# Splitting the last 4 MB store of an instance-norm kernel into 120 and 8 partitions

## The chip, the cores and the metric

The kernel runs on one core of one Trainium2 chip. The metric is device microseconds of one execution. Executions of one kernel mostly agree within 0.2% (the six of before lie within 0.13%), so a few microseconds can be told apart with several runs, and one microsecond only inside a trace. Times below are medians of the runs named, and times since the start of the span where they have four digits before the point.

## The reference

```python
x = np.random.randn(256, 256, 4096).astype(np.float32); eps = 1e-5
mean = np.mean(x, axis=2, keepdims=True)
var = np.var(x, axis=2, keepdims=True)
out = (x - mean) / np.sqrt(var + eps)
```

65536 rows of 4096 floats, each normalized by itself: 1.07 GB in, 1.07 GB out.

## The kernel before

The rows are cut into 128 tiles of 128 partitions x 4 rows x 16 KB (8 MB). Three tile buffers rotate. SyncE issues all loads and stores, VectorE and ScalarE share the arithmetic. The first and the last tile are stored in halves (2 rows of each partition, 32 KB, 4 MB in all), so that the first half leaves while the second is still computed.

```python
def take(engine, sem, count):
    engine.wait_ge(sem, count)
    engine.sem_clear(sem)

def store_half(s, t, h):                 # one DMA over all 128 partitions
    r = half_of(h)
    take(S, second(done, s, h), half)
    S.dma_start(out=out_t[t][:, r, :], in_=X[s][:, r, :]).then_inc(second(stored, s, h), 16)
# ... (cut) the end of SyncE's program:
load(last % BUFS, last)
store((last - 2) % BUFS, last - 2)
store((last - 1) % BUFS, last - 1)
store_half(last % BUFS, last, 0)
store_half(last % BUFS, last, 1)
for s in ((last - 2) % BUFS, (last - 1) % BUFS, last % BUFS, BUFS):
    take(S, stored[s], 16)
```

`last` is 127, `half` is 2, `BUFS` is 3, `K` is 4. `stored[BUFS]` counts the increments of the last half store. "Ring" below is one of the core's sixteen DMA engines with its queue of packets. An increment is what one ring adds to a DMA's semaphore when its share has landed: here 16 for each whole DMA, one per ring (4144 for the 259 transfers of before). The tiles lie in SBUF, the on-chip memory.

Two words have a narrower sense. A "port" is the place at which packets of different rings are supposed to hold one another up. And a ring's number is a name, since the traces do not number the rings: 0 to 7 are the rings of a store of 8 partitions, 15 is the one that a store of 120 leaves out, and ring k is the one that a store of k + 1 partitions has and a store of k has not. That the rings of a smaller store are among those of a larger one is assumed, not shown.

## Time and profile before

| | value | from |
|---|---|---|
| time | 4964.76 us, median of 6 (4962.69 to 4969.12) | runs beside the changed kernel |
| data moved | 2147.5 MB at 433 GB/s | the page's DMA rows |
| issue of the last store | 4943.18 | timeline |
| its sixteen increments | eight at 10.9 to 11.0 us after the issue, the last at 15.76 us | trace |
| last increment to end of span | 1.4 us | trace |

The prediction shows the lines behind these. One more view of before is needed for what follows, the rings' work after the last issue (columns: stretch, its length, busy time of VectorE, ScalarE and GpSimd, TensorE clock, share of the time that the rings held packets, and the data rate):

```profile
core 0: us, DVE busy (x) ACT busy (x) POOL busy (x), PEclk, DMA share, GB/s
4944.20:4949.00 4.80, 0.00 (x0) 0.00 (x0) 0.00 (x0) 1.00 1.00 430
4949.00:4953.80 4.80, 0.00 (x0) 0.00 (x0) 0.00 (x0) 1.00 0.90 389
4953.80:4959.00 5.20, 0.00 (x0) 0.00 (x0) 0.00 (x0) 1.00 0.18 76
```

For 9.6 us the rings are full or nearly so and move data at close to the rate of the whole body (433 GB/s); then for 5 us only stragglers work. Those 5 us are what the change goes after.

### The profile page before, as it was taken

To read this page: it belongs to the slowest core of one execution; us is meant where nothing else is said; L and a number is where in the kernel's file an instruction comes from. 1 tells how busy PE (TensorE), PEld (TensorE's weight loads), DVE (VectorE), ACT (ScalarE), POOL (GpSimd) and SP (SyncE) were. 2 spreads that over 40 slices of the span, in tenths; PEclk is the share of its full clock that TensorE was granted. 3 is DMA by queue.
4 is the path that set the end of the run, shared out by engine and by line. 5 is a ranking of instruction groups with operands and counts; after the bars stand their busy time and mean duration, and the time that the engine had idled before them with its cause. 6 is when DMAs were issued, how large, how long until landed. Compare 5 with 4: busy or idle time off the path is not lost.

```text
span 4960.3 us, 6348 instructions
## 1 busy us (share of the span) xinstructions
DVE 3390.1 (68%) x2439; ACT 2505.6 (51%) x1416; POOL 0.2 (0%) x4
## 2 busy tenths in 40 slices
DVE  6766666776677766777667776677666776677766
ACT  5555544555445544555445554455544555455545
POOL 0000000000000000000000000000000000000000
DMA  9999999999999999999999999999999999999999
GB/s 423 431 435 430 431 434 433 433 436 433 433 436 432 434 436 432 435 435 433 437 432 434 436 432 434 436 432 433 437 432 434 435 433 435 435 432 438 432 433 406
DMA packets 37299, 2147.52 MB, mean 433 GB/s; under 512 B 4144, under 2 KB 4144, under 8 KB 4144
## 3 DMA queue, kind: packets, MB, share of 16 engines
q1 hardware_dynamic: 37296, 2147.50, 100.0%
q14 instruction: 3, 0.02, 0.0%
HBM read 1073.74 MB, written 1073.74 MB: 433 GB/s over the span
## 4 chain that ended last, share of the span: by engine, by line
DMA 71%; DVE 19%; ACT 7%; another core or an unknown queue 1%; issue 1%; SPq 0%; ACTq 0%; DVEq 0%
DMA x<-in_x_dram 40%; DMA out_dram<-x 31%; DVE part L89 17%; ACT junk L132 3%; ACT x L140 3%; DVE nsum L91 1%; DVE x L110 1%; DVE nmean L93 1%; ACTq L182 0%; ACT std L137 0%; DVE nbias L102 0%; SPq L159 0%; SPq L154 0%; DVE rstd L100 0%
## 5 line engine op out<-in xcount | busy, mean ns | idle before, releaser
L89 DVE TENSOR_REDUCE part<-x 128x64 f32<-128x4096 f32 x512 | 2258.6, 4411 | 1452.4 <-DMA x<-in_x_dram 1452.4
L132 ACT ACTIVATE junk<-x,nmean 128x4096 f32<-128x4096 f32 x512 | 1883.0, 3678 | 2417.0 <-DVE nmean L93 2417.0
L110 DVE TENSOR_SCALAR x<-x,rstd,nbias 128x4096 f32<-128x4096 f32 x382 | 910.2, 2411 | 37.6 <-DVE nbias L102 16.4
L140 ACT ACTIVATE x<-x,nbias,rstd 128x4096 f32<-128x4096 f32 x130 | 492.2, 3786 | 0.0
L91 DVE TENSOR_REDUCE nsum<-part 128x1 f32<-128x64 f32 x512 | 112.4, 220 | 17.7
L132 ACT ACTIVATION_READ_ACCUMULATOR junk<-x,nmean 128x1 f32 x512 | 95.5, 186 | 0.0
L93 DVE TENSOR_SCALAR nmean<-nsum 128x1 f32<-128x1 f32 x512 | 78.5, 153 | 17.5
L100 DVE RECIPROCAL rstd<-std 128x1 f32<-128x1 f32 (+1 forms) x260 | 41.7, 160 | 17.2 <-ACT std L137 16.5
L102 DVE TENSOR_TENSOR nbias<-nmean,rstd 128x1 f32<-128x1 f32 (+1 forms) x260 | 41.6, 160 | 8.9
L137 ACT ACTIVATE std<-ss,eps_tile 128x1 f32<-128x1 f32 x130 | 38.3, 295 | 15.1
L124 ACT ACTIVATE std<-ss,eps_tile 128x3 f32<-128x3 f32 (+1 forms) x130 | 38.5, 296 | 4.2
L132 ACT ACT_TABLE_LOAD x1 | 1.3, 1283 | 1.2 <-DVE eps_tile L211 1.2
L124 ACT ACT_TABLE_LOAD x1 | 1.3, 1283 | 0.0
L211 DVE MEMSET eps_tile<- 128x1 f32 x1 | 0.1, 59 | 1.0 <-SPq L181 1.0
L248 POOL MEMSET const-uint8-127<- 128x1 uint8 x1 | 0.1, 102 | 0.0
L248 POOL MEMSET const-bfloat16-1.0<- 128x1 bf16 x1 | 0.1, 101 | 0.0
L248 POOL MEMSET const-float32-0.0<- 128x1 f32 x1 | 0.1, 98 | 0.2 <-issue 0.2
L248 POOL MEMSET const-float32-1.0<- 128x1 f32 x1 | 0.1, 98 | 0.0
## 6 DMA issues: line engine op xcount, KB each, us to landing
out_dram<-x SPq DMA_DIRECT2D x4, 4096.0 KB, 18.8
x<-in_x_dram SPq DMA_DIRECT2D x2, 4096.0 KB, 16.7
x<-in_x_dram SPq DMA_DIRECT2D x127, 49.2
out_dram<-x SPq DMA_DIRECT2D x126, 30.5
```

What stands on the lines that cost most here:

```text
L89: mine(V.tensor_reduce(out=part[s][:, r, :], in_=row, axis=AX.X, op=ALU.add))
L91: mine(V.tensor_reduce(out=nsum[s][:, c], in_=part[s][:, r, :], axis=AX.X, op=ALU.add, negate=True))
L93: V.tensor_scalar_mul(out=nmean[s][:, c], in0=nsum[s][:, c], scalar1=1.0 / d).then_inc(means, 1)
L100: mine(V.reciprocal(out=rstd[s][:, c], in_=std[s][:, c]))
L102: mine(V.tensor_mul(out=nbias[s][:, c], in0=nmean[s][:, c], in1=rstd[s][:, c]))
L110: V.tensor_scalar(out=x[:, r, :], in0=x[:, r, :], scalar1=rstd[s][:, c], scalar2=nbias[s][:, c], op0=ALU.mult, op1=ALU.add,).then_inc(dn, 1)
L124: A.activation(out=std[s][:, r0:last], in_=ss[s][:, r0:last], func=AF.Sqrt, bias=eps_tile, scale=1.0 / d).then_inc(stds, 1)
L132: A.activation(out=junk, in_=x[:, r, :], func=AF.Square, bias=nmean[s][:, c], scale=1.0, accum_out=ss[s][:, c]).then_inc(own_a, 1)
L137: A.activation(out=std[s][:, c], in_=ss[s][:, c], func=AF.Sqrt, bias=eps_tile, scale=1.0 / d).then_inc(stds, 1)
L140: A.activation(out=x[:, last - 1, :], in_=x[:, last - 1, :], func=AF.Identity, bias=nbias[s][:, c], scale=rstd[s][:, c]).then_inc(dn, 1)
L211: V.memset(eps_tile, eps).then_inc(ready, 1)
L248: nc = _bacc.Bacc("TRN2", target_bir_lowering=False, num_devices=1)
```

## The change

The intent, as I read it: one ring ends some 5 us after eight of the others. A store of 120 partitions should leave that ring out, and the 8 partitions missing go one each to eight rings that are taken to be early.

```diff
+    edge = nc.alloc_semaphore("edge")
...
                 store_half(last % BUFS, last, 0)
-                store_half(last % BUFS, last, 1)
+                take(S, done[BUFS], half)
+                for p, sem in ((slice(0, 120), stored[BUFS]), (slice(120, P), edge)):
+                    src = X[last % BUFS][p, half:K, :]
+                    S.dma_start(out=out_t[last][p, half:K, :], in_=src).then_inc(sem, 16)
+                take(S, edge, 16)
                 for s in ((last - 2) % BUFS, (last - 1) % BUFS, last % BUFS, BUFS):
                     take(S, stored[s], 16)
```

## The prediction

> **What bounds the kernel now.** I read the page's busy table and DMA rows first, then the chain of waits, then the last 60 us. The page of the kernel before:
>
> ```profile
> span 4960.3 us, 6348 instructions
> DVE 3390.1 (68%) x2439; ACT 2505.6 (51%) x1416; POOL 0.2 (0%) x4
> ...
> DMA  9999999999999999999999999999999999999999
> ...
> q1 hardware_dynamic: 37296, 2147.50, 100.0%
> ...
> HBM read 1073.74 MB, written 1073.74 MB: 433 GB/s over the span
> ```
>
> Neither compute engine is full (68% and 51%), while the sixteen DMA rings are full in every slice and their packets take 100.0% of sixteen engines' span. The kernel moves 2147.5 MB at 433 GB/s, and 2147.5 MB / 433 GB/s is 4960 us, the whole span. So the body is a pure transfer limit, which the change does not touch: the same bytes leave by the same rings. The only thing it can alter is how the last rings run out. That is the end of the program, on SyncE:
>
> ```profile
> start us, us, engine line op out<-in xcount [idle before <-releaser]
> ...
> 4940.05 2.41 DVE L110 TENSOR_SCALAR x<-x,rstd,nbias 128x4096 f32<-128x4096 f32 x1
> 4943.18 0.33 SPq L170 DMA_DIRECT2D out_dram<-x  x1
> ```
>
> ```profile
> SPq L68 <- ACT x L140: 16.5, 1, 16.5
> SPq L68 <- DMA out_dram<-x: 15.3, 2, 9.7
> ```
>
> ```profile
> issues: line engine op xcount, KB each, median us to landing
> out_dram<-x SPq DMA_DIRECT2D x1, 4096.0 KB, 15.8
> ```
>
> The last arithmetic ends near 4943.1, the last store is issued at 4943.18, and after it SyncE does nothing but wait for stores: 15.3 us in two waits, the longer 9.7 us (5.7 us for the first half of the last tile, then 9.7 us for the second). It lands 15.8 us after its issue, at 4958.94; the remaining 1.4 us to 4960.3 are closing barriers. How busy the rings are in that stretch:
>
> ```profile
> core 0: us, DVE busy (x) ACT busy (x) POOL busy (x), PEclk, DMA share, GB/s
> 4944.20:4953.80 9.60, 0.00 (x0) 0.00 (x0) 0.00 (x0) 1.00 0.95 410
> 4953.80:4954.30 0.50, 0.00 (x0) 0.00 (x0) 0.00 (x0) 1.00 0.61 262
> 4954.30:4955.80 1.50, 0.00 (x0) 0.00 (x0) 0.00 (x0) 1.00 0.20 87
> 4955.80:4957.40 1.60, 0.00 (x0) 0.00 (x0) 0.00 (x0) 1.00 0.19 82
> ```
>
> Until 4953.8 the rings are nearly all busy (0.95), then they run out one after another. No view prints single semaphore increments, but the trace records them. The sixteen increments of this store come at 4954.10 to 4954.22 (eight rings), then 4954.96, 4955.55, 4955.61, 4955.64, 4957.10, 4957.40, 4957.53 and 4958.94. So the end is one ring, 4.84 us behind the eight that had caught up and 1.41 us behind the next. Its packet records show eight packets of 32 KB back to back from 4948.79 to 4958.47, 1.21 us each, and 0.47 us to the increment; it was still draining the first half when the others started on the second. Eight rings by contrast were idle for some 3 us before the first packet of the last store at 4944.01, that is 0.83 us after its issue. Over the run one ring falls behind steadily (the last increment of a store trails the first by 1.1 us at 219 us, 6.7 us at 920 us, 7.4 us at 4630 us, 8.2 us at the last but one store). The change aims at that ring.
>
> [...] each of the 259 transfers has 16 increments, 4144 in all, the page's count of packets under 512 B. Nothing before shows 120 or 8.
> [...] The trace has one steadily late ring, but does not number the rings, so it cannot say that it is 15.
> [...] sixteen rings reach 433 GB/s together, 27 GB/s each, which is what 32 KB in 1.21 us gives; it shows no transfer of another shape.
>
> **The change part by part.**
> It removes one store of 128 partitions x 32 KB. [...]
> It adds a store of 120 partitions: fifteen rings with eight packets each, 9.7 us again; ring 15 gets none. It adds a store of 8 partitions: one packet on each of rings 0 to 7, 1.21 us more there, queued behind the first. Bytes stay 4 MB. Increments go from 16 to 15 + 8, so the count of tiny packets should rise from 4144 to 4151.
> SyncE: one more issue (the present one took 0.33 us, and the next instruction came 0.38 us after it started). The second issue at about 4943.6 comes while rings 0 to 7 have some 10 us of packets ahead of them, so it lies beside the transfer. One more wait and clear, a clear being 0.025 us in the trace, about 0.05 us, also hidden where the main store ends later.
> The path that sets the end is the last ring. With unchanged rates:
> if the late ring is 15, its end falls to that of its first half, 4949.27, and the next ring decides: 4957.53, or, if one of the three rings at 4957.1 to 4957.5 is among 0 to 7 (likely: each is with chance about one half), that plus 1.21, at most 4958.74. Gain 0.2 to 1.4 us;
> if the late ring is among 8 to 14, nothing changes, 0;
> if it is among 0 to 7, it gets a ninth packet, 4958.94 + 1.21 = 4960.15, loss 1.2 us.
> I give these 0.4, 0.25 and 0.35, since somebody who writes 120 + 8 aims at ring 15[...]. The sum is 0.4 x (-0.5) + 0 + 0.35 x 1.2 = +0.2 us: nothing.
>
> **The rivals.**
> A, ports (chance 0.35): with 120 partitions the engines may get eight neighbouring partitions each. [...] Rings that start together would share a port and each run at half rate: 19.4 us in place of 9.7. [...] Eight rings start together[...]: the end goes from 4958.94 to about 4944.0 + 19.4 + 0.4 = 4963.8, +4.8 us. The eight-partition store is worse off: [...] 4 x 1.21 = 4.8 us, not 1.21, so up to +9.7 us where both meet. I take +5 to +10, middle +7. [...]
> B, interleaved partitions (chance 0.1): if engine e takes partitions e, e+15, e+30 and so on, fifteen rings read fifteen neighbours at a time[...]. 3.93 MB at 4 x 27 GB/s is 36 us, about +27 us. That is still only 0.5% of the time.
> C, the wait moves (small): SyncE waits for the 8-partition store first and for the others after. As all waits must pass, their order changes nothing; the last landing decides. The closing barriers stay 1.4 us.
> D, the transfer is hidden anyway: it isn't for the late ring, since nothing else runs after 4943.2; but for seven of the rings there are 1.4 to 4.8 us of slack, which is what the extra packet of the eight-partition store would live in.
>
> **Range and chances.** Base 4965.49 us, three runs from 4963.85 to 4969.12, so the noise is larger than the change's sum in the plain case. Plain case (0.55): 4965.7. Ports (0.35): 4965.5 + 7 = 4972.5. Interleaved (0.1): 4992. The middle of that mixture lies a little above the base; I say 4967.0. Eight in ten: 4962.5 (full gain of 1.4 us and a good run) to 4976 (ports with both meetings). A 2% step is 99 us, six times what the whole tail after the last issue lasts (15.8 us): the change cannot take out more than that, and even the interleaved rival adds 27. Faster 0.004, same 0.991, slower 0.005.
>
> **What would show each step.** In the changed kernel's page: DMA rings still 9 in every slice and 433 GB/s; tiny packets 4151 and hardware packets 37303 if fifteen and eight rings are right (4160 and 37312 if both still use sixteen). The last part of 3840 KB should land 14.3 to 15.8 us after its issue and that of 256 KB not later than about 16.5 us in the plain case; over 20 us for either, with packets of 2.4 us in place of 1.21, would show the ports, and over 35 us the interleaving. In the increments of the 3840 KB store, no ring at 4.8 us behind would show that the late one was number 15. What would make the prediction wrong: the store of 8 partitions taking much longer than one packet per ring, a lateness that differs so much from run to run that single runs say nothing, or a different drift of the rings over the 4900 us ahead of the changed lines, which would have to be noise, since not one instruction there has changed.

## The result, and the profile after

| | before | after |
|---|---|---|
| median of 6 | 4964.76 us | 4972.54 us (4970.92 to 4973.28) |
| last store's (first) issue to its last increment | 15.76 us | 24.02 us |
| last increment to end of span | 1.4 us | 1.6 us |

The change costs 7.8 us by the medians. The ratio of the fast runs is 1.0014, with a 95% interval of 1.0001 to 1.0027: a small slowdown, far inside 2%. (A ratio is the mean time of one kernel's fast runs over that of the other's in the same rounds, so not quite the ratio of the medians.) The lines of the changed kernel's page that answer to those shown of before:

```profile
span 4970.6 us, 6350 instructions
...
DVE 3390.9 (68%) x2439; ACT 2505.5 (50%) x1416; POOL 0.2 (0%) x4
...
DMA packets 37307, 2147.52 MB, mean 432 GB/s; under 512 B 4152, under 2 KB 4152, under 8 KB 4152
...
q1 hardware_dynamic: 37303, 2147.50, 100.0%
```

Same arithmetic, same bytes, same body. The packets of the hardware queue are 37303, seven more than before: sixteen increments became fifteen and eight. (4152 small packets are those 4151 and one of the instruction queue.) The two profiled spans differ by 10.3 us and not 7.8, because this run reached the last store 1.74 us later, at 4944.92 against 4943.18, before anything that was changed: run to run noise. The tail of the changed kernel, SyncE's two issues merged, then its waits:

```profile
4944.92 1.37 SPq L210 DMA_DIRECT2D out_dram<-x  x2
```

```profile
SPq L69 <- DMA out_dram<-x: 22.7, 1, 22.7
```

```profile
issues: line engine op xcount, KB each, median us to landing
out_dram<-x SPq DMA_DIRECT2D x1, 3840.0 KB, 22.2
out_dram<-x SPq DMA_DIRECT2D x1, 256.0 KB
```

One wait of 22.7 us took the place of two of 15.3 us together. The larger part lands 22.2 us after its issue where the whole store took 15.8. (The view gives no landing for the 256 KB; the increments in the trace put it 23.56 us after its own issue.) Where the time went shows in the rings' view of the changed kernel, to be read against that of before:

```profile
core 0: us, DVE busy (x) ACT busy (x) POOL busy (x), PEclk, DMA share, GB/s
4946.00:4951.00 5.00, 0.00 (x0) 0.00 (x0) 0.00 (x0) 1.00 0.95 229
4951.00:4956.00 5.00, 0.00 (x0) 0.00 (x0) 0.00 (x0) 1.00 0.87 210
4956.00:4961.00 5.00, 0.00 (x0) 0.00 (x0) 0.00 (x0) 1.00 0.91 236
4961.00:4966.00 5.00, 0.00 (x0) 0.00 (x0) 0.00 (x0) 1.00 0.51 151
```

Until 4961 the rings hold packets 0.87 to 0.95 of the time, about as before (1.00 and 0.90), but move 210 to 236 GB/s in place of 430 and 389. The busy share alone would show no fault: a packet that crawls counts as busy. The packet records say the same. All of the last store's packets of 32 KB took 1.21 to 1.26 us before. Of the 136 packets that start after 4945.7 in the changed kernel, 52 take 2.4 to 2.6 us, 43 still 1.21 to 1.3, most others something between; four take 4.4 to 4.9 us, among them the last two of the late ring's first half (4.56 and 4.39 us).

### The profile page after: what moved, and what is told of

Read it like the earlier page. It is cut to its first block, busy times and chain, and to the rows that moved or that the text cites. A ratio compares the mean times of both kernels' runs of the same rounds, so it can differ in the third digit from the quotient of the medians.

```text
span 4970.6 us, 6350 instructions
## 1 busy us (share of the span) xinstructions
DVE 3390.9 (68%) x2439; ACT 2505.5 (50%) x1416; POOL 0.2 (0%) x4
## 2 busy tenths in 40 slices
DMA packets 37307, 2147.52 MB, mean 432 GB/s; under 512 B 4152, under 2 KB 4152, under 8 KB 4152
## 3 DMA queue, kind: packets, MB, share of 16 engines
q1 hardware_dynamic: 37303, 2147.50, 100.0%
## 4 chain that ended last, share of the span: by engine, by line
DMA 73%; DVE 18%; ACT 7%; another core or an unknown queue 1%; issue 1%; SPq 0%; ACTq 0%; DVEq 0%
DMA x<-in_x_dram 41%; DMA out_dram<-x 32%; DVE part L90 16%; ACT junk L133 3%; ACT x L141 3%; DVE nsum L92 1%; DVE nmean L94 1%; DVE x L111 0%; ACTq L183 0%; ACT std L138 0%; SPq L155 0%; SPq L160 0%; ACTq L69 0%; DVE nbias L103 0%
## 6 DMA issues: line engine op xcount, KB each, us to landing
out_dram<-x SPq DMA_DIRECT2D x1, 3840.0 KB, 22.2
x<-in_x_dram SPq DMA_DIRECT2D x127, 49.2
out_dram<-x SPq DMA_DIRECT2D x126, 30.5
```

## The experiments

The theory, the prediction's rival A (called PORT in the expectations): with 120 partitions rings meet in pairs at a port, and each runs at half rate. Against it stand the memory side (the rows that a ring writes also changed), the count (a store on fewer than sixteen rings, the nine packets where eight were, or a second issue and semaphore), and the question whether there is a late ring 15 at all. All eleven kernels gave correct results.

**One shape at a time (m1_shapes).** Behind all waits of the kernel before, ten transfers, each waited for. The first and second write wrong rows, later ones put them right.

```diff
+    for src, dst in ((0:32:4, 120:128), (120:128, 0:128:16), (120:128, 120:128), (0:16:4, 0:4),
+                     (0:4, 0:4), (0:64, 0:64), (0:120, 0:120), (0:128, 0:128)):     # written out one by one
+        S.dma_start(out=out_t[last][dst, half:K, :], in_=X[last % BUFS][src, half:K, :]).then_inc(edge, 16)
+        take(S, edge, 16)
+    # then loads of 0:128 and 0:120 into the same buffer, in the same way
```

> After all stores of the kernel before have landed, ten single transfers run one at a time, each waited for, rings otherwise idle; each packet is 32 KB, 1.21 us alone, and a landing costs some 1.3 us on top (0.83 us to the first packet, about 0.4 after the last). Three theories. PORT[...]: 8 partitions in steps of 4[...] 2.5 us; partitions 120-127 to spread rows 6.1; partitions 120-127 to their own rows 6.1; 4 partitions in steps of 4 2.5; partitions 0-3 6.1; partitions 0-63 11; 0-119 20.7; all 128 11 us. MEMORY (the rows of the HBM side decide, not the partitions): first 6.1, second 2.5, third 6.1. COUNT (what costs is a store on fewer than sixteen rings, or its issue, and a packet is always 1.21 us): every store of 4 or 8 partitions about 2.5, 0-63 6.2, 0-119 11, all 128 11 us. The two loads at the end, 128 and 120 partitions: 11 and 11 if only reads of SBUF suffer, 11 and about 20 if writes do too.

SyncE's timeline in this kernel; since each transfer is waited for, the distance from one start to the next is the time that it took, with some 0.1 us for the wait:

```profile
start us, us, engine line op out<-in xcount [idle before <-releaser]
...
4959.60 0.81 SPq L209 DMA_DIRECT2D out_dram<-x  x1
4962.71 0.31 SPq L211 DMA_DIRECT2D out_dram<-x  x1
4969.07 0.28 SPq L213 DMA_DIRECT2D out_dram<-x  x1
4975.39 0.64 SPq L215 DMA_DIRECT2D out_dram<-x  x1
4978.34 0.26 SPq L217 DMA_DIRECT2D out_dram<-x  x1
4984.62 0.55 SPq L219 DMA_DIRECT2D out_dram<-x  x1
4996.61 0.34 SPq L221 DMA_DIRECT2D out_dram<-x  x1
5017.86 0.37 SPq L223 DMA_DIRECT2D out_dram<-x  x1
5029.08 0.37 SPq L225 DMA_DIRECT2D x<-in_x_dram  x1
5041.55 0.35 SPq L227 DMA_DIRECT2D x<-in_x_dram  x1
```

With the last increments and packet times of the trace:

| transfer | PORT expected, us | issue to last increment, us | packets of 32 KB, us |
|---|---|---|---|
| 8 partitions in steps of 4, to neighbouring rows | 2.5 | 3.03 | 1.21 |
| partitions 120-127, to spread rows | 6.1 | 6.28 | 4.7 to 5.1 |
| partitions 120-127, to their own rows | 6.1 | 6.26 | 4.7 to 5.1 |
| 4 partitions in steps of 4 | 2.5 | 2.88 | 1.21 |
| partitions 0-3 | 6.1 | 6.21 | 4.7 to 4.9 |
| partitions 0-63 (2 MB) | 11 | 11.92 | 2.4 to 2.6 |
| partitions 0-119 | 20.7 | 21.14 | mostly 2.4 to 2.6 |
| all 128 (4 MB) | 11 | 11.13 | 1.21 to 1.26 |
| load of all 128 | 11 | 12.35 | mostly 1.21 |
| load of 0-119 | 11 or 20 | 22.01 | mostly 2.3 to 2.6 |

The same number of packets on the same number of rings takes 3.03 or 6.26 us, depending on the partitions alone; where the rows lie in memory changes nothing (6.28 and 6.26), and neighbouring rows written from spread partitions are fast (3.03). For stores, that rules out the memory side and the count. Half the data (0-63) takes longer than all of it. The load of 120 partitions is slow too, but not in quite the way that the store is (see the next run). The two stepped transfers came out 0.4 to 0.5 us over the expectation, which fits their longer issue (0.64 and 0.81 us, against 0.26 to 0.31).

**Which partitions share (m2_pairs).** Two partitions, two rings, one packet each.

```diff
+    for src in (0:64:32, 0:128:64, 0:8:4, 0:2):       # written out one by one, each waited for
+        S.dma_start(out=out_t[last][0:2, half:K, :], in_=X[last % BUFS][src, half:K, :]).then_inc(edge, 16)
+        take(S, edge, 16)
```

> After all stores of the kernel before, four stores of two partitions (two rings, 32 KB each, one packet per ring), one at a time, all to the same two rows. [...] PORT[...]: partitions 0 and 32 share a port, packets 2.4 to 2.6 us, landing about 4 us; 0 and 64 do not, 1.21 us, landing 2.9; 0 and 4 do not, 2.9; 0 and 1 do, 4. If only neighbouring partitions share (ports of eight partitions in a row): 0 and 32 would be 1.21 us like 0 and 64, and 0 and 4 would be 2.4.

Partitions 0 and 32 took packets of 2.51 and 2.53 us; 0 and 64 took 1.21 and 1.22; 0 and 4 took 1.21 both; 0 and 1 took 2.51 and 2.53. So of the four pairs tried, two (0 with 32, 0 with 1) hold each other to half rate and two (0 with 64, 0 with 4) do not.

Which partitions each ring of a store of 120 reads, and so which rings meet in it, no view shows. The trace of the isolated 120 shows that not all of them do: one increment came 11.61 us after the issue, with packets of 1.21 to 1.73 us, while the other fourteen came after 19.87 to 21.14. Why just one ring was spared is not shown. The load of 0-119 has no such ring: all fifteen increments came after 21.48 to 22.01 us. So the load is not slow in quite the way that the store is; why it is slow stays open.

(The run of before on this chip gave 5005.0 us, a single one of unknown state; nothing here rests on total times.)

**The 120 without the 8 (e1_edge_after).**

```diff
     # 120 partitions as in the change, then all four waits for stores, then:
+    S.dma_start(out=out_t[last][120:P, half:K, :], in_=X[last % BUFS][120:P, half:K, :]).then_inc(edge, 16)
+    take(S, edge, 16)
```

> The store of 120 partitions alone at the end, and the one of 8 partitions only after all others have landed. PORT: the 120-partition store still lands 20 to 22 us after its issue, packets of about 2.4 us among it, and the 8 partitions take 6 us by themselves on top: about 12 us over before. COUNT or the two stores disturbing one another: 120 partitions land within 16 us, as the whole one did, and the 8 take 2.5 us: about 3 us over before.

The 120 partitions landed 21.04 us after their issue, against 15.76 for the whole store of before; the 8, alone, took 6.26 us. The profiled run was 4974.67 us, 11 us over the median of before in these rounds (4963.7, seven runs). The four runs scatter (4973.74 to 5010.16), for a reason that I did not find, so the ratio (1.0055, 1.0021 to 1.0088) says only "slower". What follows from the trace: the store of 120 lands some 5 us late without the 8 behind it.

**The 8 without the 120 (e2_whole_and_edge).** The second store has the partitions and the size of the change's but belongs to the tile before, whose bytes it writes a second time.

```diff
+    take(S, stored[(last - 1) % BUFS], 16)
     store_half(last % BUFS, last, 1)
+    S.dma_start(out=out_t[last - 1][120:P, half:K, :], in_=X[(last - 1) % BUFS][120:P, half:K, :]).then_inc(edge, 16)
+    take(S, edge, 16)
```

> The whole store of 128 partitions, then a second store of 8 partitions (120-127, 32 KB each) of the tile before, done twice with the same bytes: the second store of the change without the first one's 120. PORT: seven rings find their ninth packet while the late one is still at work[...]; the end moves by one packet of the late ring, 1.2 to 2.5 us over before (0 to 1 if the late ring is not among 0 to 7). If the 8-partition store or its issue (0.9 us) were what costs, +6 to +8 us, as in the change.

The whole store's last increment came at 4960.63 and the small one's at 4961.85, 1.22 us later: one packet of a late ring. Three of the four runs lay at 4964.65 to 4965.30 us (the fourth, 4987.36, stands alone), against 4963.7 for before: +1 to +2 us, and the ratio's interval (0.9995 to 1.0042) includes no change. As expected, the small store costs about a packet (1.22 us), and the last ring is one of 0 to 7, or it would have had no ninth packet.

**Two halves of the partitions, two halves of the rows (e3_64_64, e4_rows).** Both put two DMAs in place of the last one, with the second semaphore and wait of the change.

```diff
-    for p, sem in ((slice(0, 120), stored[BUFS]), (slice(120, P), edge)):      # the change
+    for p, sem in ((slice(0, 64), stored[BUFS]), (slice(64, P), edge)):        # e3_64_64
+    for r, sem in ((slice(half, half + 1), stored[BUFS]), (slice(half + 1, K), edge)):   # e4_rows
+        S.dma_start(out=out_t[last][:, r, :], in_=X[last % BUFS][:, r, :]).then_inc(sem, 16)   # e4_rows
```

> The last 4 MB store in two of 64 partitions, both on sixteen rings, four packets per ring each, no ring left out or given more. PORT: [...]rings that start together need 4 x 2.55 us twice, 20.4 us in place of 9.7; the end moves by +5 to +10 us, as in the change, though ring counts are those of before. COUNT (fewer than sixteen rings, or uneven packets): no loss, within 1 us of before.

> The last 4 MB store in two of 128 partitions, one row of 16 KB per partition each: two issues, two semaphores and one more wait as in the change[...]. PORT: nothing lost, last landing 15.5 to 16.5 us after the first issue, time within 1 us of before. If two stores in place of one were what costs: +5 us or more.

SyncE's wait for stores at the end, first with halves of the partitions, then with halves of the rows:

```profile
SPq L69 <- DMA out_dram<-x: 22.8, 1, 22.8
```

```profile
SPq L69 <- DMA out_dram<-x: 15.0, 1, 15.0
```

64 and 64: 4974.53 us against 4963.28 in the same rounds (ratio 1.0026, 1.0010 to 1.0043), last increment 24.0 us after the first issue. Sixteen rings, four packets each and four again, nothing left out, and the last landing is as late as in the change (24.02). The first half's increments came mostly 11.4 to 12.0 us after the first issue, the second's mostly 21.0 to 21.7: each half took about as long as a whole store does alone (11.13 in m1_shapes, where 0-63 took 11.92). By the medians the loss is 11.3 us against the change's 7.8; two of the four runs lie at 4971.80 and 4971.96, 8.5 us over before. Rows: 4963.39 us against 4963.28 (1.0000, 0.9984 to 1.0017), last increment 15.76 us after the first issue, as before to the hundredth. Two issues, a second semaphore and one more wait cost nothing that can be seen; cutting the partitions costs.

**Which ring is late (e5_tags, e6_tags, e9_tags).** Behind the whole last store, four stores of 512 B per partition over n partitions of a tile that has long landed. Each lands with the latest of its rings. The traces have n increments from rings for each of them; which rings these are they do not show.

```diff
+    take(S, stored[(last - 2) % BUFS], 16)
     store_half(last % BUFS, last, 1)
+    for i, (n, sem) in enumerate(zip((1, 2, 4, 8), tags)):       # e6: (5, 6, 7, 8); e9: (3, 4, 5, 8)
+        src = X[(last - 2) % BUFS][0:n, i, 0:128]
+        S.dma_start(out=out_t[last - 2][0:n, i, 0:128], in_=src).then_inc(sem, 16)
```

> The whole last store of the kernel before, followed by four stores of 512 B per partition of an older tile, over 1, 2, 4 and 8 partitions. [...] PORT theory with the late ring among 0 to 7 (what the packet chains of the changed kernel suggest): one of the four is the first late one, by 4 to 9 us after the earliest. If the change's idea (ring 15 is late) were right: none late. Time within 2 us of before.

> As the tags of before, now over 5, 6, 7 and 8 partitions behind the whole last store. The late ring of the first tag run lay among rings 4 to 7. If it is ring 7, the stores of 5, 6 and 7 partitions land with the others and only that of 8 lands several us late; if it is another one, an earlier store is late too; if the late ring changes from run to run, none may be.

> As the tags of before, over 3, 4, 5 and 8 partitions behind the whole last store. In the first tag run the late ring lay among 4 to 7, in the second among 0 to 4; if it is one and the same ring it is number 4: the stores of 3 and 4 partitions land with the earlier rings and those of 5 and 8 end with the late one. If it changes from run to run, anything else; ring 15 is late only if none of the four is.

| run | whole store's last increment | last increment of the tag over n partitions | late ring |
|---|---|---|---|
| first | 4960.32 | n=4: 4957.36; n=8: 4960.50 | 4 to 7 |
| second | 4961.78 | n=5: 4961.96; n=6, 7, 8: 4962.15 to 4962.50 | 0 to 4 |
| third | 4961.18 | n=3: 4955.94; n=4: 4960.53; n=5: 4961.36 | 4 |

The first tag that reaches the late ring ends 0.18 to 0.19 us after the store's last increment in all three. In the third the late ring is in the store of 5 partitions and not in that of 4, which is what ring 4 means here; the other two allow it; they ran on three chips. In the second the expectation that it is ring 7 fell. In no run is it 15: the tag over 8 partitions in the first, and that over 5 in the other two, end with it. That all three have the same ring is not shown, only not contradicted. These numbers rest on the assumption that the rings of a smaller tag are among those of a larger one.

**The same split in every store (e7_all_120_8, e8_all_64_64).** To see whether the loss belongs to the tail, where rings start together after a gap, the split was put into all 126 whole-tile stores.

```diff
     def store(s, t):
         take(S, done[s], K)
-        S.dma_start(out=rows_of(out_t, t), in_=X[s][:, :, :]).then_inc(stored[s], 16)
+        for p, sem in ((slice(0, 120), stored[s]), (slice(120, P), edges[s])):      # e8: 64 in place of 120
+            S.dma_start(out=rows_of(out_t, t)[p], in_=X[s][p, :, :]).then_inc(sem, 16)
     # loads wait for edges[s] too; the last half stores are those of before
```

> Every whole-tile store of the kernel (126 of 8 MB) split into 120 and 8 partitions. PORT: a store alone would take 20 us more each, 126 times, 2520 us at most (7480 us in all); part of it is lost again where one ring of a pair loads while the other stores. I expect 5500 to 7000 us. If the loss were a thing of the tail alone (rings starting together after an idle gap), or the rings of a pair settled out of step: 5000 to 5200 us, ring 0 to 7 having nine packets where they had eight in the stores.

> Every whole-tile store split into 64 and 64 partitions: all on sixteen rings, every ring the same number of packets as before. PORT: about as slow as the split into 120 and 8 in every store (6972 us), 6000 to 7400 us. If the loss there came from rings left out and unevenly loaded: within 2% of before.

120 and 8 everywhere: 6971.61 us, 40% over before (4963.28 in the same rounds). 64 and 64 everywhere: 7221.49 us (45% over that 4963.28, 44% over the single run of before in its own rounds, 5005.0). Each is one run of unknown state; the losses are far larger than any scatter seen here. Two stretches in the body, first of before, then of 120 and 8 everywhere:

```profile
1000.00:2000.00 1000.00, 684.97 (x489) 502.82 (x284) 0.00 (x0) 1.00 1.00 434
3000.00:4000.00 1000.00, 684.83 (x492) 503.15 (x285) 0.00 (x0) 1.00 1.00 434
```

```profile
1000.00:2000.00 1000.00, 477.31 (x342) 350.79 (x198) 0.00 (x0) 1.00 0.94 303
3000.00:4000.00 1000.00, 495.27 (x358) 366.59 (x208) 0.00 (x0) 1.00 0.94 314
```

The share of busy rings falls from 1.00 to 0.94, the data rate from 434 to some 310 GB/s. The rings do not settle out of step. Packets of 64 KB took 2.42 us on the mean before and 3.21 us here (3.50 with 64 and 64). In the issues of 120 and 8 everywhere, loads slow down too, though their shape is unchanged, presumably since they queue on the same rings (argued, not tested apart); before it was 30.5 for the stores and 49.2 for the loads:

```profile
issues: line engine op xcount, KB each, median us to landing
...
out_dram<-x SPq DMA_DIRECT2D x252, 57.3
x<-in_x_dram SPq DMA_DIRECT2D x127, 72.8
```

No run splits every store by rows, so that two stores in place of one cost nothing is shown for the last store only. The longer packets say that the rate of the rings is what was lost.

## Why the prediction was right or wrong

The time, 4972.54 us, lies in the range (4962.5 to 4976.0), and nearly at the value of rival A (4972.5). The single number, 4967.0, was a middle between cases and lies 5.5 us low; weighted by its own chances the three cases give 0.55 x 4965.7 + 0.35 x 4972.5 + 0.1 x 4992 = 4970.7. That rival A's value is met to a tenth is luck, as the steps show: one term of it was too small, another too large. Step by step:

- **The bound.** Right: compute times, bytes and ring share are unchanged, and all of the difference lies behind the last issue.
- **Fifteen and eight rings.** Right: 37303 hardware packets, as foretold, not 37312.
- **"With unchanged rates".** Wrong, and this was the case given the most weight (0.55). Of the changed kernel's last 136 packets 52 took 2.4 to 2.6 us where 1.21 was assumed; the stores measured singly show that partitions alone decide this (3.03 or 6.26 us for eight packets), and the pairs show it for two packets (2.51 and 2.53 us, or 1.21).
- **The late ring, 0.4 for number 15.** Wrong. The whole-and-8 run puts the last ring among 0 to 7 (a ninth packet, 1.22 us later), and the tags put it at 4 in the one run that can tell. The change spares a ring that is not late and hands the late one a ninth packet. Nor does that ring fall behind "steadily": the spread of a store's increments grows to 6.7 us by some 800 us, stays near 6.8 until about 4390, and then grows to 8.2.
- **Rival A, the 120 partitions.** Right in sign, and in size for fourteen of the rings; the slow packets are shown, the port behind them is not. It said that the rings would end at 4963.8, 20.6 us after an issue at 4943.18. Fourteen of the fifteen increments came by 21.08 us after the issue. The isolated store of 120 takes 10.0 us longer than that of 128 (21.14 against 11.13); only about half of it shows in the kernel, because the whole store's tail already waited for a straggler until 15.76.
- **Rival A, the late ring while the others start.** Missing from the sum. The late ring still drained the first half store when the others began on the 120: the last increment of the first half moved from 23.0 us after its issue to 29.45 us (27.62 in the run with the 8 partitions afterwards). The chain of this ring's packets is the path that ended last: six of the first half took 1.21 to 1.24 us, the last two 4.56 and 4.39, then all eight of its share of the 120 took 1.21 again, and the ninth 1.83. So the 6.45 us that its first half lost are the whole of the 6.46 us by which the 120 landed later, and the half rate of the other rings, which ended at 21.08, did not set the end. That the other rings stretched it is argued from its packets of 4.4 and 4.6 us, close to the 4.7 to 5.1 us of the eight neighbours 120-127 in the isolated run. No run took the other rings away with the late ring left alone. Its 22.22 us is the last increment of the 120.
- **Rival A, the 8 partitions.** Right sign, size off: up to +4.8 us was allowed, and the last increment came 1.80 us after that of the 120. The eight increments are spread from 4957.56 to 4968.94, so few of the packets can overlap; started together, eight take 6.26 us against 3.03. Sum: 15.76 to 22.22 is 6.46 us for the 120, 1.80 more for the 8, 8.26 us in this trace, against "middle +7" and 7.8 us in the medians.
- **Rival B, interleaved partitions.** Ruled out: 81 of the 120 packets of the isolated store took 2.4 to 2.6 us, as partitions 0 and 32 together do (2.51 and 2.53), one ring kept nearly its full rate (packets of 1.21 to 1.73 us), and the store landed after 21.14 us, not 36 (an estimate that gave fifteen neighbours the rate of four rings; the eight of 120-127 took 4.7 to 5.1 us for a packet each, about the rate of two).
- **Rival C, the moved wait.** Nearly right. It said that the order of waits changes nothing. As the 8 partitions land last and are waited for first, four waits and clears come behind the last landing, and the end lies 1.6 us after it in place of 1.4, as it does with 64 and 64 and with rows, which have the same order of waits.

No version here beats the kernel before; the split by rows equals it. To take work from the late ring alone one would have to spare it, ring 4 in the one run that can tell, and the ring that the 120 leave out is another: the late one took eight of the 120 packets. Another way to spare it was not tried; the most that one could gain is the 1.41 us to the next ring.

## What to carry to other kernels

If a DMA must be cut, cut it along the free dimension (here the rows of each partition) and keep all 128 partitions in each piece: in the last store here two pieces by rows cost nothing (4963.39 us against 4963.28) and two pieces by partitions moved 210 to 236 GB/s in place of 430 and 389; cut by partitions throughout, the kernel took 40 to 45% longer (6971.61 and 7221.49 us against 4963.28). Read the data rate beside the busy share of the rings: at those 210 to 236 GB/s the share was still 0.87 to 0.95. Before work is taken from a straggling ring, find out which ring it is, and what the pieces do to it: here the straggler itself slowed down while they ran (two packets of 4.56 and 4.39 us where the others of its half took 1.21 to 1.24), and that set the end.
